# One pair of PSUM pools for the whole program, and the way down over output tiles q and 4 + q

## The chip, the cores and the metric

The kernel runs on one core of a Trainium2 chip. The metric is the device time of one execution in microseconds (us). The kernel before takes 1079.97 us in the median of three runs (1079.96 to 1080.04).

## The reference

One layer of a hybrid decoder on a sequence of 1024 positions of width 1024, all in float32. A mixer (a short convolution on 512 channels, chunkwise retention with four heads on the others) is followed by a squared-ReLU network; both add to the residual stream, and a norm ends the layer:

```python
for _ in range(DEPTH):
    h = h + hybrid_mixer(rms_norm(h, norm1_g), w_in, conv_w, conv_norm_g, ret_norm_g, w_out)
    h = h + sq_relu_mlp(rms_norm(h, norm2_g), w_up, w_down)
return rms_norm(h, final_norm_g)

def sq_relu_mlp(u, w_up, w_down):
    hdn = jax.nn.relu(u @ w_up)
    return (hdn * hdn) @ w_down
```

`w_up` is 1024 x 4096 and `w_down` 4096 x 1024.

## The kernel before

Everything is held transposed: features on the 128 partitions, the 1024 positions along the columns, in two halves of 512 (`hs[0]` low, `hs[1]` high). The residual stream is eight tiles `x2[0..7]` of 128 x 1024, one for each 128 features.

**Matmuls.** float32 operands are split in a high part and the rest (`wh`, `wl` for weights, `U`, `V`, `hid` for the moving side), and a product is three matmuls for each block of 128 features: high by high, high by rest, rest by high. ACT casts the high part, DVE (sometimes POOL) subtracts for the rest. A product of four blocks is 12 matmuls of 512 columns into one PSUM bank; the code is `mm` (line 395), `product` (772) and, for the way down, `down_product` (1266).

**Fewer products.** Both matrix products of the network use a scheme of seven products instead of eight (Winograd's form of Strassen's), on 2 x 2 blocks of weights and data. The sums of weight blocks are made on POOL (`r<-r,r` in the profile, from `Left.split`), those of data blocks on DVE and POOL. For the way down, the four quarters of a 2 x 2 block of outputs are two tiles of `x2` by two halves of the positions. The seven products are added straight into these quarters by DVE (`down_take`, line 1277), in a basis in which fewer additions are needed. For that the residual has to be put in the basis first (`new_basis`, line 1001, two subtractions on POOL for each pair of tiles) and taken out at the end (one addition to each of the two tiles, lines 1316 and 1346). Before the change, the pairs are neighbours: (0, 1), (2, 3), (4, 5), (6, 7).

**Stages around the change.** The program is recorded by hand (a manual schedule): each engine runs its instructions in the order of the code, and waits are put in where data or buffers need them.

1. Output projection, `group(j)` (1057), j = 0 to 3: eight products each, for output tiles j and 4 + j. The finished tiles go to `x2` (`out_evac`), and the network's input blocks are made from them, step by step (`group_todo`, 1035; a step is one product, the table `todo` counts 8 steps to a group). Tiles of `x2` that are not needed for a while are written to HBM (`put_aside`, 1025; `k<-x` on SP's queue) and later read back (`fetch_back`, 1031; `x<-k`).
2. The early products (1248): the 14 products of the first two pairs of up blocks, without a way down beside them. The table `rest` says what is issued beside each. The norm's roots are matmuls with a column of ones (L311), and the rows are spread over the partitions with L337 into two banks that are kept for the rest of the program (`r_half`).
3. The loop (1328): up products (L401) and down products (L1274) in turn, then the last block of `w_down` and the final norm (1377 on).

**Banks.** PSUM has eight banks for this kernel. Up to the end of the projection two pools, `pm` and `pr`, have four each. Then both are closed and three are opened: two banks for the up products (`pu`, which takes the name `pm`), four for the down products (`pd`, taking the name `pr`), two for the norm rows (`pn`). A bank is given again when the last reader of its old tile is done.

In the profile nearly all work of DVE, ACT and POOL has line L74, since one helper records it; the tiles' names tell the operations apart: `x<-x,b` adds a bank to the residual, `t<-t,b` adds an up product, `wl<-r,wh` is the rest of a weight piece, `U<-un,U` and `V<-t,V` the rest of a data block, `x<-x,x` and `x<-x` the two subtractions of `new_basis`, `t<-t,t` on POOL sums of squares (before 452 us) or sums of data blocks.

Of the kernel before, what the change touches and what calls it, by code (L numbers as in the profile page):

```python
# [14 lines left out]
PSUM = bass.MemoryType.PSUM  # L15
# [64 lines left out]
def hybrid_layer(  # L80
# [18 lines left out]
    pool = Engine(nc.gpsimd, 0.2, 2.5, now, clock)  # L99
# [5 lines left out]
    rw = ctx.enter_context(tc.tile_pool(name="rw", bufs=4))  # L105
    wp = ctx.enter_context(tc.tile_pool(name="wp", bufs=4))
    mixer = ctx.enter_context(ExitStack())
    banks_ = ctx.enter_context(ExitStack())
    pm = banks_.enter_context(tc.tile_pool(name="pm", bufs=4, space=PSUM))
    pr = banks_.enter_context(tc.tile_pool(name="pr", bufs=4, space=PSUM))  # L110
    tp = mixer.enter_context(tc.tile_pool(name="tp", bufs=6))
    xp = mixer.enter_context(tc.tile_pool(name="xp", bufs=1))

# [4 lines left out]
    def nm(s):  # L118
        n_[0] += 1
        return f"{s}{n_[0]}"  # L120

    def unit(dt=F32, s="u"):
        return big.tile([P, T], dt, tag="u", name=nm(s))
# [6 lines left out]
    def bank(pool_=None):  # L130
        return (pool_ or pm).tile([P, H], F32, tag="b", name=nm("b"))
# [4 lines left out]
    hs = [slice(0, H), slice(H, T)]  # L136
# [196 lines left out]
    def spread(wide, pool_=None):  # L333

        b = bank(pool_ or pr)[:, : len(wide) * P]
        for c, d in enumerate(wide):
            nc.tensor.matmul(b[:, c * P : (c + 1) * P], d, ident, start=True, stop=True)  # L337
        return b
# [201 lines left out]
    def rot_tiles(ct, st):  # L540

        ac, as_ = unit(s="ac"), unit(s="as")

        def evac_a(A):
            for half, sl in enumerate(hs):
                dve.tensor_mul(ac[:, sl], A[half], ct[:, sl])
                dve.tensor_mul(as_[:, sl], A[half], st[:, sl])

        tile_in(evac_a)
        q = [unit(s="q") for _ in range(2)]  # L550

        def evac(B):
            for half, sl in enumerate(hs):
                t2, t3 = tmp(), tmp()
                dve.tensor_mul(t2, B[half], st[:, sl])
                dve.tensor_mul(t3, B[half], ct[:, sl])
                lo_, up_ = slice(0, 64), slice(64, 128)
                pool.tensor_sub(q[0][lo_, sl], ac[lo_, sl], t2[lo_])
                dve.tensor_sub(q[1][lo_, sl], ac[up_, sl], t2[up_])
                dve.tensor_add(q[0][up_, sl], t3[lo_], as_[lo_, sl])  # L560
                pool.tensor_add(q[1][up_, sl], t3[up_], as_[up_, sl])

        tile_in(evac)
        return q
# [189 lines left out]
    for p in range(2):  # L754
        q = rot_tiles(*ropes)
# [11 lines left out]
    def put_hi(name, j, src):  # L767
        u = unit(F32R, "U")
        act.copy(u[:, :H], src)
        U.setdefault(name, [None] * 4)[j] = (u[:, :H], u[:, H:])  # L770
# [44 lines left out]
    for j in range(4):  # L815
        for c, name in ((0, "11"), (1, "21"), (2, "22")):
            k = j + (4 if c else 0)
            sl = hs[c == 2]
# [119 lines left out]
    x2 = [unit(s="x2") for _ in range(KT)]  # L938
# [59 lines left out]
                un[i] = unit(s="un")  # L998
            act.activation(un[i][:, hs[half]], x, AF.Copy, scale=g)

    def new_basis(i):


        for f, part in ((i - 1, hs[1]), (i, hs[0])):
            pool.tensor_sub(x2[f][:, part], x2[f][:, part], x2[i][:, hs[1]])

# [16 lines left out]
    def put_aside(i):  # L1025

        aside[i] = kept.tile([P, T], F32, tag="k", name=nm("k"))
        nc.sync.dma_start(aside[i], x2[i])
        x2[i] = None
# [5 lines left out]
    def group_todo(j):  # L1035

        hi_of = lambda *names: [lambda x=x: put_hi(x, j, source(x, j)) for x in names]
        lo_of = lambda *names: [lambda x=x: put_lo(x, j, source(x, j)) for x in names]
        todo = {
            2: [lambda: put_scaled_hi("11", j, j, 0)],  # L1040
            3: [lambda: put_scaled_lo("11", j, j, 0)],
            4: [lambda: put_scaled_hi("21", j, 4 + j, 0)],
            5: [lambda: put_scaled_lo("21", j, 4 + j, 0)],
            8: [lambda: sum1(j)] + hi_of("t1"),
            9: lo_of("t1") + [lambda: sum3(j)],
            10: [lambda: sum2(j)],
        }
        if j < 3:
            todo[10] += hi_of("t3")
            todo[11] = lo_of("t3") + hi_of("t2")  # L1050
            todo[12] = lo_of("t2") + [lambda: put_scaled_hi("22", j, 4 + j, 1)]
            todo[13] = [lambda: put_scaled_lo("22", j, 4 + j, 1), lambda: sum4(j)] + hi_of("t4")
            todo[14] = lo_of("t4")
            todo[15] = [lambda: put_aside(4 + j)]
        return todo

    def group(j):
# [27 lines left out]
    todo = {}  # L1085
    for j in range(4):
        for at, fs in group_todo(j).items():
            todo.setdefault(8 * j + at, []).extend(fs)
    todo[16] += [lambda: new_basis(1)]
    todo[17] += [lambda: put_aside(0), lambda: put_aside(1)]  # L1090
    todo[24] += [lambda: put_aside(2)]
    for j in range(4):
        group(j)
    banks_.close()
    pm = ctx.enter_context(tc.tile_pool(name="pu", bufs=2, space=PSUM))
    pr = ctx.enter_context(tc.tile_pool(name="pd", bufs=4, space=PSUM))
    pn = ctx.enter_context(tc.tile_pool(name="pn", bufs=2, space=PSUM))

    blocks = [w_up[p, i] for p in range(EARLY, NP_) for i in range(4)]
    blocks += [w_last[i] for i in range(KT)]  # L1100
# [45 lines left out]
    r_half, waiting = [None, None], []  # L1146
# [42 lines left out]
    def v_split(pairs, n, j):  # L1189
        c = pairs[j].c  # L1190
        src = c[{1: "11", 2: "21", 3: "22", 4: "21", 5: "11", 6: "11", 7: "12"}[n]]
        u = unit(F32R, "V")
        act.copy(u[:, :H], src)
        eng = pool if j and n not in (2,5) else dve
        eng.tensor_sub(u[:, H:], src, f32(u[:, :H]))
        V.setdefault(n, [None] * 2)[j] = (u[:, :H], u[:, H:])
# [26 lines left out]
    def call(f, *js):  # L1223
        return [lambda j=j: f(j) for j in js]
# [4 lines left out]
    def lo22(j):  # L1229
# [7 lines left out]
        lo("t4", dve, 3) + call(fetch_back, 2, 4, 5, 6),  # L1237
        [],
        [],
        call(new_basis, 7),  # L1240
        call(new_basis, 5),
        call(new_basis, 3),
        [lambda: v_split(early, 1, 0)],
        [lambda: v_split(early, 1, 1)],
        [],
# [2 lines left out]
    for at, (n, p) in enumerate((n, p) for n in MLP_ORDER for p in range(EARLY)):  # L1248
        b = early[p].product(n)
        if at == 0:  # L1250
            up.fetch(4)
        prepare()
        for f in rest[at]:
            f()
        put_now()
        early[p].take(n, b)
        if at == 3:
            roots = [token_roots([sums_[h]], rtok[:, 4 * h : 4 * h + 4]) for h in range(2)]
        if at == 5:
            wides = [rnorms(r) for r in roots]  # L1260
        if at == 8:
            r_half[:] = [spread(w, pn) for w in wides]
        while r_half[0] is not None and waiting:
            waiting.pop(0)()

# [11 lines left out]
    def down_take(n, h, bs):  # L1277
        for i, b in enumerate(bs):
            q = 2 * h + i
            quads = [x2[2 * q + f][:, sl] for f in range(2) for sl in hs]  # L1280
            for to, op in {
                1: ((0, ALU.add), (3, ALU.add)), 2: ((0, ALU.add),), 3: ((1, ALU.add),),
                4: ((2, ALU.add),), 5: ((2, ALU.subtract), (3, ALU.add)), 6: ((3, ALU.add),),
                7: ((1, ALU.subtract), (3, ALU.add)),
            }[n]:
                dve.tensor_tensor(quads[to], quads[to], b, op)
# [11 lines left out]
    def jobs(b, old, new):  # L1298

        todo = []  # L1300
        for k, n in enumerate(DOWN_ORDER):
            four = [[] for _ in range(4)]
            if k < 6:
                for j in range(2):
                    four[j].append(lambda n=DOWN_ORDER[k + 1], j=j: v_split(old, n, j))
                    four[j + 1].append(lambda n=DOWN_ORDER[k + 1], j=j: v_next(old, n, j))
            elif b < NBLK - 2:
                for j in range(2):
                    four[j].append(lambda j=j: v_both(new, 1, j))
            if b == NBLK - 2:  # L1310
                late = {4: ((0, "11"), (0, "21"), (0, "12"), (0, "22")), 5: ((1, "11"),)}.get(k, ())
                for f, x in zip(four, late):
                    f.append(lambda x=x: last_split(*x))
                if k == 6:
                    for q in range(4):
                        x = x2[2 * q + 1]
                        four[q].append(
                            lambda x=x: pool.tensor_add(x[:, hs[0]], x[:, hs[0]], x[:, hs[1]])
                        )
                    for f, name in ((four[0], "12"), (four[2], "22"), (four[3], "21")):  # L1320
                        f.append(lambda name=name: last_split(1, name))
            todo += four
        return todo
# [4 lines left out]
    for b in range(NBLK - 1):  # L1328
        new = [Pair(pm), Pair(pm)]
        todo = jobs(b, pairs, new)  # L1330
# [12 lines left out]
            else:  # L1343
                pairs[x].take(y, bk)
    for q in range(4):
        pool.tensor_add(x2[2 * q][:, hs[1]], x2[2 * q][:, hs[1]], x2[2 * q + 1][:, hs[1]])


    wd = []
# [27 lines left out]
    for sl in (slice(0, 512), slice(512, 768), slice(768, 1024)):  # L1377
# [3 lines left out]
        for i in range(KT):  # L1381
# [21 lines left out]
            x = x2[i][:, sl]  # L1403
# [120 lines left out]
```

## Time and profile before

| | |
|---|---|
| median of 3 runs | 1079.97 us |
| the profiled execution | 1082.14 us |
| its span (first to last instruction) | 1080.3 us |
| granted TensorE clock, mean | 0.995 |
| output projection on PE | 353.7 to 440.6 us |
| early products | 441 to 484 us |
| loop, then last block and final norm | 484 to 1022, to 1080 us |

DVE is TensorE's companion at 82% of the span, but in the second half of it the page's 40 slices show DVE at 90% or more nearly everywhere. A row of the timeline gives the start and the length in us, the engine, the line, the tile written and the tiles read, the shapes and a count, and in brackets the idle time ahead of it with what ended it. A row of the groups gives a count, the busy time and the mean in ns. A row of the windows gives the busy time of PE, of its weight loads, of DVE, ACT and POOL in a stretch, then the granted clock.

### The profile page before, as it was taken

To read this page: it belongs to the slowest core of one execution; us is meant where nothing else is said; L and a number is where in the kernel's file an instruction comes from. 1 tells how busy PE (TensorE), PEld (TensorE's weight loads), DVE (VectorE), ACT (ScalarE), POOL (GpSimd) and SP (SyncE) were. 2 spreads that over 40 slices of the span, in tenths; PEclk is the share of its full clock that TensorE was granted. 3 is DMA by queue.
4 is the path that set the end of the run, shared out by engine and by line. 5 is a ranking of instruction groups with operands and counts; after the bars stand their busy time and mean duration, and the time that the engine had idled before them with its cause. 6 is when DMAs were issued, how large, how long until landed. Compare 5 with 4: busy or idle time off the path is not lost.

```text
span 1080.3 us, 14040 instructions
## 1 busy us (share of the span) xinstructions
PE 1060.6 (98%) x4936; PEld 882.7 (82%) x4936; DVE 881.2 (82%) x1255; ACT 463.3 (43%) x916; POOL 540.3 (50%) x370
## 2 busy tenths in 40 slices
PE   9999999999999999999999999999999999999996
PEld 7888888887778888788788888888888888888886
DVE  8446546799997666699999989999899899899945
ACT  8211445763335544444343443443343434334453
POOL 6233323256752132559548258267286295384543
PEclk9999999999999999999999999999999999999998
DMA  7121121212223635050121211211301211210204
GB/s 273 62 59 48 31 79 69 100 58 77 69 59 117 224 114 169 2 194 30 58 69 39 79 39 49 89 25 54 93 25 50 88 30 43 85 30 12 77 1 157
DMA packets 40311, 81.75 MB, mean 76 GB/s; under 512 B 4528, under 2 KB 6704, under 8 KB 40240
## 3 DMA queue, kind: packets, MB, share of 16 engines
q1 hardware_dynamic: 40240, 80.85, 23.2%
q8 instruction: 39, 0.64, 0.2%
q14 instruction: 32, 0.26, 0.1%
HBM read 71.40 MB, written 9.44 MB: 75 GB/s over the span
## 4 chain that ended last, share of the span: by engine, by line
PE 80%; DVE 11%; issue 3%; POOL 3%; ACT 2%; DMA 1%; POOLq 0%; DVEq 0%; SPq 0%; ACTq 0%
PE b L401 50%; PE b L1274 23%; PE b L355 4%; DVE z L74 2%; DVE wl L74 2%; POOL r L74 1%; POOL z L74 1%; DVE t L74 1%; DVE x L74 1%; DVE xs L74 1%; DVE U L74 1%; DVE q L74 1%; ACT h L74 1%; PE b L337 1%; DVE m L74 1%
## 5 line engine op out<-in xcount | busy, mean ns | idle before, releaser
L401 PE MATMUL b<-U,wh 128*128 128x512 f32 x1024 | 315.9, 390 | 2.4 <-DVE x L74 1.2
L74 ACT CAST wh<-r 128x512 fp32r<-128x512 f32 x286 | 175.9, 620 | 321.2 <-PE b L401 134.7
L74 DVE TENSOR_TENSOR wl<-r,wh 128x512 fp32r<-128x512 f32 x251 | 233.3, 932 | 90.9 <-ACT wh L74 90.0
L74 POOL TENSOR_TENSOR r<-r,r 128x512 f32<-128x512 f32 x136 | 209.8, 1545 | 116.0 <-DVE wl L74 65.6
L1274 PE MATMUL b<-V,wh 128*128 128x512 f32 x784 | 242.0, 389 | 0.7 <-POOL V L74 0.4
L401 PEld LDWEIGHTS b<-U,wh 128*128 128x128 f32 x1024 | 191.8, 188 | 43.4 <-issue 2.8
L74 DVE TENSOR_TENSOR x<-x,b 128x512 f32<-128x512 f32 (+1 forms) x320 | 197.8, 663 | 24.4 <-PE b L401 19.3
L401 PE MATMUL b<-U,wl 128*128 128x512 f32 x512 | 199.4, 389 | 0.0
L1274 PEld LDWEIGHTS b<-V,wh 128*128 128x128 f32 x784 | 147.0, 188 | 32.3 <-POOL V L74 0.8
L74 POOL TENSOR_TENSOR t<-t,t 128x512 f32<-128x512 f32 x70 | 106.3, 1523 | 97.9 <-ACT t L74 51.9
L1274 PE MATMUL b<-V,wl 128*128 128x512 f32 x392 | 152.5, 389 | 0.0
L74 POOL TENSOR_TENSOR wl<-r,wh 128x512 fp32r<-128x512 f32 x35 | 49.1, 1408 | 159.2 <-ACT wh L74 151.9
L401 PEld LDWEIGHTS b<-U,wl 128*128 128x128 f32 x512 | 96.0, 188 | 20.7 <-POOL wl L74 0.4
L401 PE MATMUL b<-uh,wh 128*128 128x512 f32 x304 | 103.3, 399 | 2.3 <-DVE z L74 2.3
L401 PE MATMUL b<-uh,wl 128*128 128x512 f32 x304 | 100.8, 392 | 1.1 <-DVE wl L74 1.1
L401 PE MATMUL b<-ul,wh 128*128 128x512 f32 x304 | 101.0, 392 | 0.0
L1274 PEld LDWEIGHTS b<-V,wl 128*128 128x128 f32 x392 | 73.6, 188 | 15.2
L74 POOL TENSOR_TENSOR V<-t,V 128x512 fp32r<-128x512 f32 x35 | 49.6, 1417 | 67.2 <-ACT V L74 67.2
L74 DVE TENSOR_TENSOR t<-t,b 128x512 f32<-128x512 f32 x112 | 75.8, 677 | 1.7 <-POOL t L74 1.2
L74 ACT ACTIVATE t<-t 128x512 f32<-128x512 f32 x64 | 40.2, 631 | 81.9 <-DVE t L74 81.3
L74 DVE TENSOR_TENSOR V<-t,V 128x512 fp32r<-128x512 f32 x63 | 70.3, 1116 | 0.0
L401 PEld LDWEIGHTS b<-uh,wl 128*128 128x128 f32 x304 | 57.3, 189 | 13.9 <-DVE wl L74 1.5
(168 smaller groups left out, 1431.0 us busy)
## 6 DMA issues: line engine op xcount, KB each, us to landing
r<-w_up_t SPq DMA_DIRECT2D x64, 256.0 KB, 2.6
r<-w_down_t SPq DMA_DIRECT2D x56, 256.0 KB, 2.7
r<-w_in_t SPq DMA_DIRECT2D x48, 256.0 KB, 2.6
xt<-xT SPq DMA_DIRECT2D x16, 256.0 KB, 5.4
xs<-xT SPq DMA_DIRECT2D x8, 512.0 KB, 4.8
r<-w_out_t SPq DMA_DIRECT2D x16, 256.0 KB, 2.7
x<-xT SPq DMA_DIRECT2D x8, 512.0 KB, 7.4
k<-x SPq DMA_DIRECT2D x6, 512.0 KB, 3.2
```

What stands on the lines that cost most here:

```text
L74: return f(out, *args, **kw)
L337: nc.tensor.matmul(b[:, c * P : (c + 1) * P], d, ident, start=True, stop=True)
L355: nc.tensor.matmul(vb[i], a[k][:, i * P : (i + 1) * P], b[k // 2][:, vs], start=(k == 0 and a is uh and b is vh), stop=(k == KT - 1 and a ...
L401: nc.tensor.matmul(b, a[:, k, :], rhs(n, k)[r], start=(start and i == 0), stop=(stop and i == len(ops) - 1),)
L1274: nc.tensor.matmul(b, a, r, start=(i == 0), stop=(i == len(ops) - 1))
```

## The change

The two pools `pm` and `pr` of four banks stay for the whole program; the norm rows take two banks of `pm`. The way down pairs output tiles q and 4 + q instead of 2q and 2q + 1: these come from the same group of the projection, so `new_basis(j)` can stand behind the group's own steps, at step 14 (which is six products into the next group), and tiles j and 4 + j are put aside together at step 15. Only the last pair (3, 7), which is never put aside, stays in the early products. The columns of `w_down` are laid out on the host to match.

```diff
-    banks_ = ctx.enter_context(ExitStack())
-    pm = banks_.enter_context(tc.tile_pool(name="pm", bufs=4, space=PSUM))
-    pr = banks_.enter_context(tc.tile_pool(name="pr", bufs=4, space=PSUM))
+    pm = ctx.enter_context(tc.tile_pool(name="pm", bufs=4, space=PSUM))
+    pr = ctx.enter_context(tc.tile_pool(name="pr", bufs=4, space=PSUM))
...
-    def new_basis(i):
-        for f, part in ((i - 1, hs[1]), (i, hs[0])):
-            pool.tensor_sub(x2[f][:, part], x2[f][:, part], x2[i][:, hs[1]])
+    def new_basis(j):
+        for f, part in ((j, hs[1]), (4 + j, hs[0])):
+            pool.tensor_sub(x2[f][:, part], x2[f][:, part], x2[4 + j][:, hs[1]])
...
             todo[14] = lo_of("t4")
-            todo[15] = [lambda: put_aside(4 + j)]
+            todo[14] += [lambda: new_basis(j)]
+            todo[15] = [lambda: put_aside(j), lambda: put_aside(4 + j)]
...
-    todo[16] += [lambda: new_basis(1)]
-    todo[17] += [lambda: put_aside(0), lambda: put_aside(1)]
-    todo[24] += [lambda: put_aside(2)]
...
-    banks_.close()
-    pm = ctx.enter_context(tc.tile_pool(name="pu", bufs=2, space=PSUM))
-    pr = ctx.enter_context(tc.tile_pool(name="pd", bufs=4, space=PSUM))
-    pn = ctx.enter_context(tc.tile_pool(name="pn", bufs=2, space=PSUM))
...
-        call(new_basis, 7),
-        call(new_basis, 5),
         call(new_basis, 3),
+        [],
+        [],
...
-            r_half[:] = [spread(w, pn) for w in wides]
+            r_half[:] = [spread(w, pm) for w in wides]
...
-            quads = [x2[2 * q + f][:, sl] for f in range(2) for sl in hs]
+            quads = [x2[4 * f + q][:, sl] for f in range(2) for sl in hs]
...
-                        x = x2[2 * q + 1]
+                        x = x2[4 + q]
...
-        pool.tensor_add(x2[2 * q][:, hs[1]], x2[2 * q][:, hs[1]], x2[2 * q + 1][:, hs[1]])
+        pool.tensor_add(x2[q][:, hs[1]], x2[q][:, hs[1]], x2[4 + q][:, hs[1]])
```

Where instructions move, on POOL, at the end of the projection and in the first four early products (`t_3190` sums squares, `r` are weight blocks, `x_3164` and `x_3168` are x2[2] and x2[6]; a piece of the difference):

```order
 L74 TENSOR_TENSOR t_3190<-t_3190,t_3846 128x512
-L74 TENSOR_TENSOR r_3594<-r_3594,r_3596 128x512
-L74 TENSOR_TENSOR r_3590<-r_3594,r_3590 128x512
-L74 TENSOR_TENSOR r_3592<-r_3592,r_3590 128x512
-L74 TENSOR_TENSOR t_3190<-t_3190,t_3871 128x512
+L74 TENSOR_TENSOR x_3164<-x_3164,x_3168 128x512
+L74 TENSOR_TENSOR x_3168<-x_3168 128x512
+L74 TENSOR_TENSOR r_3592<-r_3592,r_3594 128x512
+L74 TENSOR_TENSOR r_3588<-r_3592,r_3588 128x512
+L74 TENSOR_TENSOR r_3590<-r_3590,r_3588 128x512
+L74 TENSOR_TENSOR t_3190<-t_3190,t_3873 128x512
```

The two subtractions of the pair (2, 6) come in ahead of the three weight sums and of the last addition of squares (`t_3190`), which are otherwise the same.

On POOL again, later in the early products, before the change (`x_4037` and `x_3169` are x2[6], read back, and x2[7]; the next two pairs are (4, 5) and (2, 3); `V_4214` is a data block of the first down product):

```order
L74 TENSOR_TENSOR r_3594<-r_3596,r_3590 128x512
L74 TENSOR_TENSOR x_4037<-x_4037,x_3169 128x512
L74 TENSOR_TENSOR x_3169<-x_3169 128x512
L74 TENSOR_TENSOR x_4033<-x_4033,x_4035 128x512
L74 TENSOR_TENSOR x_4035<-x_4035 128x512
L74 TENSOR_TENSOR x_4031<-x_4031,x_3165 128x512
L74 TENSOR_TENSOR x_3165<-x_3165 128x512
L74 TENSOR_TENSOR V_4214<-t_3997,V_4214 128x512
```

And at the same place now (`x_3165` and `x_3169` are x2[3] and x2[7], neither of them read back):

```order
L74 TENSOR_TENSOR r_3410<-r_3412,r_3406 128x512
L74 TENSOR_TENSOR r_3592<-r_3594,r_3588 128x512
L74 TENSOR_TENSOR x_3165<-x_3165,x_3169 128x512
L74 TENSOR_TENSOR x_3169<-x_3169 128x512
L74 TENSOR_TENSOR V_4203<-t_3990,V_4203 128x512
```

Four of the six subtractions have gone from here, and none of the two left reads a tile that comes back from HBM.

On PE, at the first early product, with the engines that the program waits for, before:

```order
L401 MATMUL b_3804<-yh_3080,wl_3697 128x512
L401 MATMUL b_3887<-U_3249,wh_3795 128x512 [waits DVE_49,PE_49,Activation_49]
L401 MATMUL b_3887<-U_3249,wh_3795 128x512
L401 MATMUL b_3887<-U_3249,wl_3796 128x512
L401 MATMUL b_3887<-U_3404,wh_3795 128x512 x2
```

and now:

```order
L400 MATMUL b_3804<-yh_3080,wl_3697 128x512
L400 MATMUL b_3880<-U_3249,wh_3795 128x512 [waits Activation_49]
L400 MATMUL b_3880<-U_3249,wh_3795 128x512
L400 MATMUL b_3880<-U_3249,wl_3796 128x512 [waits DVE_49]
L400 MATMUL b_3880<-U_3404,wh_3795 128x512 x2
```

The first row is the projection's last matmul. The product's first wait for DVE (and for PE's own last product) is gone, and a wait for DVE stands at the first use of `wl`; the second early product changes in the same way.

More of the change, by code (lines that the diff above doesn't have):

```diff
@@ L1502 @@
         .reshape(NBLK - 1, 2, 2, P, 2, 2, 2, P)
-        .transpose(0, 6, 2, 4, 3, 5, 1, 7)
+        .transpose(0, 4, 2, 5, 3, 6, 1, 7)
         .reshape(NBLK - 1, 4, 2, P, 4, P),
```

## The prediction

> **What bounds the kernel now.** I read the page's busy times first, then TensorE's (PE's) idle gaps in order of time, then the engines that end them.
>
> ```profile
> span 1080.3 us, 14040 instructions
> PE 1060.6 (98%) x4936; PEld 882.7 (82%) x4936; DVE 881.2 (82%) x1255; ACT 463.3 (43%) x916; POOL 540.3 (50%) x370
> 529.98 2.72 PE b L401 x12
> ```
>
> PE is busy for 98% of the span. A product of the program is 12 matmuls of 512 columns, and in the chain of work that ended last one takes 2.72 us, or 0.23 us a matmul. The time can fall only where PE is kept from this pace, and rise only where a new wait breaks it. Between 332 us (the output projection's start) and 988 us the timeline has five gaps on PE, all between 440 and 525 us, which is where the change acts.
>
> The first two, from the timeline of PE:
>
> ```profile
> 440.39 0.39 PE L401 MATMUL b<-yh,wl 128*128 128x512 f32 x1
> 441.25 0.70 PE L401 MATMUL b<-U,wh 128*128 128x512 f32 x2 [0.47 <-DVE x L74]
> 443.82 0.39 PE L401 MATMUL b<-U,wl 128*128 128x512 f32 x1
> 444.91 0.70 PE L401 MATMUL b<-U,wh 128*128 128x512 f32 x2 [0.70 <-DVE x L74]
> 447.75 0.39 PE L401 MATMUL b<-U,wh 128*128 128x512 f32 x1
> ```
>
> The last projection matmul starts at 440.39, so the first early product was due at 440.62 and the third at 440.62 + 2 x 2.72 = 446.06. It starts at 447.75: **1.69 us lost**. Both waits end with DVE's `x += b`, which empties a projection bank. The program's waits agree: these two matmuls alone name DVE and PE beside ACT, because the pools are closed there and new ones laid over the same banks.
>
> The other three:
>
> ```profile
> 494.92 0.39 PE L401 MATMUL b<-U,wh 128*128 128x512 f32 x1
> 506.44 0.70 PE L401 MATMUL b<-U,wh 128*128 128x512 f32 x2 [0.48 <-ACT wh L74]
> 520.54 0.70 PE L1274 MATMUL b<-V,wh 128*128 128x512 f32 x2 [0.25 <-DVE x L74]
> 524.25 0.70 PE L401 MATMUL b<-U,wh 128*128 128x512 f32 x2 [0.71 <-ACT t L74]
> 527.10 0.39 PE L1274 MATMUL b<-V,wh 128*128 128x512 f32 x1
> L401 PE MATMUL b<-U,wh 128*128 128x512 f32 x48 | 15.0, 393 | 1.2 <-ACT t L74 0.7 <-ACT wh L74 0.5
> 505.62 0.67 DVE L74 TENSOR_TENSOR t<-t,b 128x512 f32<-128x512 f32 x1
> 523.43 0.68 DVE L74 TENSOR_TENSOR t<-t,b 128x512 f32<-128x512 f32 x1
> ```
>
> From 494.92 to 527.10 there are 32.18 us. The group row, of this window, counts 48 `U,wh` matmuls, 8 to an up product, so six up products and the five down products between them: 11 x 2.72 = 29.92. **2.26 us lost.** The profile names ACT, but the bank decides: an up product needs the bank of the up product before last, and DVE frees those with the two `t<-t,b`, at 506.29 and 524.11, just ahead of the gaps' ends. DVE lags PE here; 0.6 to 0.9 us less lag would end these gaps.
>
> **Why DVE lags.**
>
> ```profile
> 473.71 1.28 POOL L74 TENSOR_TENSOR x<-x,x 128x512 f32<-128x512 f32 x1 [12.17 <-DMA x<-k]
> 482.56 1.76 POOL L74 TENSOR_TENSOR V<-t,V 128x512 fp32r<-128x512 f32 x1
> 479.10 0.62 ACT L74 CAST V<-t 128x512 fp32r<-128x512 f32 x1
> 473.79 1.76 DVE L74 TENSOR_TENSOR wl<-r,wh 128x512 fp32r<-128x512 f32 x1 [0.90 <-ACT wh L74]
> 478.42 1.78 DVE L74 TENSOR_TENSOR V<-t,V 128x512 fp32r<-128x512 f32 x1
> 474.00:484.00 10.00, 10.00 (x45) 8.29 (x45) 9.90 (x11) 5.29 (x10) 10.00 (x7) 1.00 0.25 74
> 451.22 0.69 DVE L74 TENSOR_TENSOR wl<-r,wh 128x512 fp32r<-128x512 f32 x1 [2.30 <-ACT wh L74]
> ```
>
> The six `new_basis` subtractions of the late pairs fill POOL from 473.71 to 482.56, after 12.17 us of waiting for a tile from HBM. Meanwhile DVE's `wl` takes 1.76 us, and 0.69 at 451.22 with POOL idle. From 474 to 484 both engines count as busy throughout (9.90 and 10.00). A POOL operation alone takes 1.28, beside DVE 1.74; a DVE operation with both inputs in SBUF that meets one ends about 0.6 behind it. Those that read a bank (`t<-t,b`, 0.67) don't mind.
>
> **The change, part by part.**
>
> *The banks.* Without close and reopen, the first early products take banks emptied groups ago and wait for weights alone (split before 440). Both gaps go: **-1.69 us**. In the loop nothing changes: the norm rows now sit in two of `pm`'s four banks, leaving two for the up products, as before.
>
> *The new order on POOL.* The count is the same (8 subtractions). Two pairs move ahead of 440. From 335 to 440 PE is busy for all of 105 us and POOL for 32.27 (first row below), so I cost them at nothing. The third pair (x2[2], x2[6]) lands in the busiest place:
>
> ```profile
> 335.00:440.00 105.00, 105.00 (x465) 86.95 (x464) 67.66 (x91) 49.98 (x86) 32.27 (x22) 1.00 0.39 131
> ...
> 441.88 1.74 POOL L74 TENSOR_TENSOR t<-t,t 128x512 f32<-128x512 f32 x1
> 443.58 4.80 POOL L74 TENSOR_TENSOR r<-r,r 128x512 f32<-128x512 f32 x3
> 448.33 1.74 POOL L74 TENSOR_TENSOR t<-t,t 128x512 f32<-128x512 f32 x1
> 451.83 0.68 DVE L74 TENSOR_TENSOR U<-un,U 128x512 fp32r<-128x512 f32 x1
> 452.44 1.41 DVE L74 SCALAR_TENSOR_TENSOR un<-x,sm,un 128x512 f32<-128x512 f32 x2
> 455.53 0.69 DVE L74 TENSOR_TENSOR wl<-r,wh 128x512 fp32r<-128x512 f32 x1 [1.69 <-ACT wh L74]
> 456.14 0.68 DVE L74 TENSOR_TENSOR U<-un,U 128x512 fp32r<-128x512 f32 x1
> 453.19 1.84 PE L311 MATMUL b<-ones,t 128*128 128x1 f32 x16
> 457.07 0.62 PE L401 MATMUL b<-U,wh 128*128 128x512 f32 x2
> ```
>
> Behind the `t` at 441.88 two subtractions go in, one beside DVE and one alone (1.74 + 1.28 = 3.0), so the three `r` and the last sum `t` run 3.0 later: `t` ends at 450.07 + 3.0 = 453.1. Two things wait for that. The sums on PE (L311), due at 453.19 - 1.69 = 451.50, need `t` for their second half. And DVE: with POOL idle from 450.07 it ran `U` at 451.83 in 0.68; now `U` meets `t` and ends 0.6 behind it, 453.7 instead of 452.5, **1.2 late**. The two `un`, ACT's `U`, `t` and `wh`, then `wl` and `U` (456.14) follow one another without slack, so the last `U`, low half of the fourth tile of "t2", ends at 456.82 + 1.2 = 458.0. The tenth and eleventh matmuls of product 6 of pair 0 (457.07 and 457.30) use that tile, the eleventh its low half; it had 0.5 to spare and now runs at 458.05, 0.75 later than before. So PE waits there until all of the 1.69 is gone and **0.75 us more**: bounds are 0 after the gain (the stretch hidden) and +2.8 (DVE loses the turn at U and both `un`, 3 x 1.1, less 0.5). I take 0.75, by the rows themselves. The roots at L311 are hidden under this wait.
>
> For this cost the Trainium skill has a rule: SBUF — State Buffer, section "SBUF: two separate sides", says of the port pair that DVE and GpSimd share that it is "an exclusive lock, not a bandwidth split", held for the whole instruction. The two full rows of 474 to 484 agree. If the engines shared evenly instead, `U` and what follows would be some 0.6 late instead of 1.2, and the sum below would be 0.6 lower; the rule speaks against this place for the pair.
>
> *The last pair* (x2[3], x2[7]) never leaves SBUF, so it doesn't wait for HBM: it follows the `r` of 459.81, at about 462.7 to 466.
>
> ```profile
> 459.81 1.74 POOL L74 TENSOR_TENSOR r<-r,r 128x512 f32<-128x512 f32 x1 [1.83 <-DVE wl L74]
> 463.32 0.69 DVE L74 TENSOR_TENSOR wl<-r,wh 128x512 fp32r<-128x512 f32 x1 [0.63 <-ACT wh L74]
> 466.37 0.39 PE L401 MATMUL b<-U,wl 128*128 128x512 f32 x1
> ```
>
> DVE's `wl` of 463.32 may lose 1.2 to the chain above and 1.1 to this pair; it ends at 464.01, PE uses it at 466.37 and comes 0.75 later too, so 3.1 us hide it. I cost it at nothing; without that cover it would be up to 1.1.
>
> *What goes after 473.* POOL is empty until `V`, which starts when ACT's `V` is there (479.72, and 0.75 later with PE): 480.5 instead of 482.56, 2.1 earlier. On DVE two `wl` and a `V` between 473.79 and 480 shrink by 1.1 each, 3.3; it comes there some 1.6 later (the 1.2, and part of the pair at 463), so it is 1.7 ahead. With PE 0.75 later its lag is 2.4 less, against 0.9 needed. The three gaps go: **-2.26 us**, bounds 0 and 2.26.
>
> *Queues and tail.* SP's writes of x2[2] and x2[6] now wait for POOL until about 446, and four `w_up` loads stand behind them:
>
> ```profile
> 422.55 1.91 SPq L160 DMA_DIRECT2D r<-w_up_t  x4
> 475.90 0.63 ACT L74 CAST wh<-r 128x512 fp32r<-128x512 f32 x1 [0.56 <-ACT t L74]
> 1022.62 6.40 POOL L74 TENSOR_TENSOR x<-x,x 128x512 f32<-128x512 f32 x4
> 1044.30 0.42 DVE L74 TENSOR_TENSOR x<-x,b 128x256 f32<-128x256 f32 x1 [0.75 <-POOL ssq L74]
> ```
>
> They are issued at about 447 instead of 422.55 and used first at 475.90: hidden, with over 20 us left. In the tail, POOL's four closing additions end at 1029 and their half is read from 1044.30: nothing either way.
>
> **The sum.** -1.69 + (1.69 + 0.75) - 2.26 = -1.5 us. The profiled execution took 1082.14 (span 1080.3), the runs 1079.97 in the median; 1.5 off gives 1080.6 for such an execution and **1078.5** for the median. A measurement here tells about 0.2%, 2.16 us, from no change.
>
> **Rivals.**
> - *The pair on POOL is hidden.* If POOL gets through by 451.8 or DVE goes first, product 6 doesn't wait: -1.69 - 2.26 = -3.95, 1076.0. For it: 0.5 us of spare at 457.30, and durations on POOL are rough. Against it: POOL has no idle time from 440.64 to 450.07 to take 3.0 in.
> - *The lag stays.* DVE is full from 474 to 515 whatever runs beside it; if `V` and the `r` on POOL only close up, the gaps at 506 to 524 remain: +0.75, 1080.7.
> - *Slower.* The same lock, lost at `U` and both `un`, which needs POOL busy until 456: +2.8 at 457.30, and with DVE that much behind the later gaps stay: 1082.8. It decides from the point where the eleventh matmul of product 6 starts after 459.5 by the old clock. Against it: behind `t` POOL's next `r` waits for DVE's own `wl` (455.53).
> - *The banks were not the wait.* Then 441 and 444 stay, but PE waits for the same `U` at 458.05 and the sum is -1.5 again.
>
> **Chances.** Forecast (with the last rival) 0.52, own range 1077.6 to 1079.6; hidden 0.20; lag stays 0.18; slower 0.10. The range 1075.8 to 1081.4 takes in all but the slower case and the far ends. Faster by over 0.2%: the hidden case and a little of the forecast, 0.26; within: 0.64; slower: 0.10.
>
> **What would show it.** PE without gaps at 441 and 444, then one gap of 1.5 to 2.5 us inside product 6 put down to DVE's `U`, and none from 500 to 527; POOL with `x` rows near 443.6 and 463 and none at 473 to 482; `t` ending near 453. It is wrong if product 6 doesn't wait, if the gaps at 506 to 524 stand, or if PE stops anywhere in 332 to 440 or in the tail where it didn't.

## The result, and the profile after

| | before | after |
|---|---|---|
| median | 1080.34 us (20 runs) | 1082.55 us (20 runs) |
| the profiled execution | 1082.14 us | 1081.98 us |
| its span | 1080.3 us | 1080.2 us |

The ratio of the times is 1.0017, interval [1.0011, 1.0024]: about 0.2% **slower**, where 0.14% faster was forecast. The two profiled executions took the same time, so they can't be compared as wholes: before's lies 1.8 us above its median. They can be compared stretch by stretch, between matmuls that both kernels have. From the timeline of PE, after (columns as above):

```profile
318.33 0.50 PE L400 MATMUL b<-uh,wh 128*128 128x512 f32 x1 [2.29 <-DVE z L74]
438.62 0.39 PE L400 MATMUL b<-yh,wl 128*128 128x512 f32 x1
449.50 0.39 PE L400 MATMUL b<-U,wl 128*128 128x512 f32 x1
449.73 0.95 PE L310 MATMUL b<-ones,t 128*128 128x1 f32 x8
453.72 1.86 PE L310 MATMUL b<-ones,t 128*128 128x1 f32 x8 [3.04 <-POOL t L74]
455.44 1.20 PE L400 MATMUL b<-U,wh 128*128 128x512 f32 x2
...
459.43 0.82 PE L400 MATMUL b<-U,wh 128*128 128x512 f32 x2
489.33 0.62 PE L1267 MATMUL b<-V,wh 128*128 128x512 f32 x2
1061.42 0.28 PE L310 MATMUL b<-ones,ssq 128*128 128x1 f32 x2
```

And the same places before, as far as not shown yet:

```profile
318.60 0.80 PE L401 MATMUL b<-uh,wh 128*128 128x512 f32 x1 [2.27 <-DVE z L74]
486.76 0.62 PE L1274 MATMUL b<-V,wh 128*128 128x512 f32 x2
1061.09 0.28 PE L311 MATMUL b<-ones,ssq 128*128 128x1 f32 x2
```

| stretch, from start to start | before | after | |
|---|---|---|---|
| z's matmul to the projection's last matmul | 121.79 | 120.29 | -1.50 |
| to the first down product (**early stretch**) | 46.37 | 50.71 | +4.34 |
| to the final norm's sums at 1061 (**the rest**) | 574.33 | 572.09 | -2.24 |

The first row is not the change: in before's execution PE ran at half pace for 3.4 us behind its wait for z (0.80 us for the first matmul in its row, 0.50 after). That came and went from profile to profile, whatever the kernel (last section). The other two rows add up: +4.34 - 2.24 = +2.1 us, which is the difference of the medians, 2.2. So the gain that was hoped for behind the early products came, and the early products lost twice as much.

What PE does there, from the windows of after:

```profile
440.00:460.00 20.00, 16.96 (x71) 14.23 (x70) 13.85 (x14) 8.26 (x15) 13.83 (x9) 0.83 0.31 107
500.00:527.00 27.00, 27.00 (x121) 22.37 (x120) 25.74 (x37) 10.82 (x19) 20.74 (x14) 1.00 0.20 59
452.50:453.00 0.50, 0.00 (x0) 0.00 (x0) 0.50 (x2) 0.00 (x0) 0.50 (x1) 1.00 0.68 262
453.00:453.50 0.50, 0.00 (x0) 0.00 (x0) 0.50 (x1) 0.00 (x0) 0.50 (x1) 0.51 0.07 25
```

The gaps at 441 and 445 are gone, and so are those from 500 to 527 (27.00 of 27.00). In their place PE stands still for 3.04 us at the roots, behind the last sum of squares `t`. While it stands the granted clock falls from 1.00 to 0.50 (at 453.0; it is back before 460), so that product 6, which follows, starts at half pace.

Behind that stop, ACT, DVE, POOL and SP of after:

```profile
427.32 0.61 ACT L74 CAST U<-un 128x512 fp32r<-128x512 f32 x1
431.34 0.73 ACT L74 ACTIVATE U<-x,sm 128x512 fp32r<-128x512 f32 x1 [3.41 <-PE b L400]
431.97 0.61 ACT L74 ACTIVATE t<-x 128x512 f32<-128x512 f32 x1
434.50 1.78 DVE L74 TENSOR_TENSOR U<-un,U 128x512 fp32r<-128x512 f32 x1
436.20 1.78 DVE L74 TENSOR_TENSOR wl<-r,wh 128x512 fp32r<-128x512 f32 x1
452.47 1.75 DVE L74 TENSOR_TENSOR U<-un,U 128x512 fp32r<-128x512 f32 x1
457.83 0.68 DVE L74 TENSOR_TENSOR U<-un,U 128x512 fp32r<-128x512 f32 x1
433.99 3.44 POOL L74 TENSOR_TENSOR r<-r,r 128x512 f32<-128x512 f32 x2
451.95 1.71 POOL L74 TENSOR_TENSOR t<-t,t 128x512 f32<-128x512 f32 x1
420.60 27.01 SPq L1027 DMA_DIRECT2D k<-x  x4
```

and of before, at the first and the last of these places:

```profile
429.60 0.72 ACT L74 ACTIVATE U<-x,sm 128x512 fp32r<-128x512 f32 x1
430.66 0.63 ACT L74 ACTIVATE t<-x 128x512 f32<-128x512 f32 x1 [0.34 <-DVE x L74]
434.89 0.68 DVE L74 TENSOR_TENSOR U<-un,U 128x512 fp32r<-128x512 f32 x1
408.30 13.85 SPq L1028 DMA_DIRECT2D k<-x  x3
```

The last row, DVE's `U` of 457.83, is the `U` of product 6 on which the prediction turned. It ends at 458.51, 19.89 us behind the start of the projection's last matmul (438.62); before it ended at 456.82, 16.43 behind 440.39. So it is **3.46 us later, where 1.2 was forecast**. One part is the forecast one (`U` at 452.47 takes 1.75 beside POOL, not 0.68). The other starts twenty microseconds earlier: ACT's `U<-x,sm` waits 3.41 us, with the square `t` behind it in ACT's queue; POOL's weight sums `r`, which follow that square's addition, come later for it and meet DVE's `U` and `wl` (1.78 each). That `U` of 434.50 ends at -2.34 us from the projection's last matmul, where before's, of 434.89, ended at -4.82: 2.5 us of the delay are there already, before POOL's two subtractions begin.

### The profile page after: what moved, and what is told of

Its sections match the earlier page's. It is cut to its first block, busy times and chain, and to the rows that moved or that the text cites. A ratio compares the mean times of both kernels' runs of the same rounds, so it can differ in the third digit from the quotient of the medians.

```text
span 1080.2 us, 14041 instructions
## 1 busy us (share of the span) xinstructions
PE 1061.0 (98%) x4936; PEld 884.6 (82%) x4936; DVE 882.9 (82%) x1255; ACT 463.8 (43%) x916; POOL 541.3 (50%) x370
## 4 chain that ended last, share of the span: by engine, by line
PE 85%; DVE 6%; POOL 4%; issue 3%; ACT 1%; DMA 0%; POOLq 0%; DVEq 0%; ACTq 0%
PE b L400 53%; PE b L1267 24%; PE b L354 4%; POOL r L74 1%; POOL z L74 1%; DVE z L74 1%; DVE wl L74 1%; DVE q L74 1%; DVE t L74 1%; PE b L336 1%; PE b L310 1%; PE b L622 0%; PE b L592 0%; DVE cv L74 0%; ACT h L74 0%
## 5 line engine op out<-in xcount | busy, mean ns | idle before, releaser
L74 DVE TENSOR_TENSOR V<-t,V 128x512 fp32r<-128x512 f32 x63 | 68.1, 1081 | 0.0
```

What stands on the lines that cost most here:

```text
L74: return f(out, *args, **kw)
```

## The experiments

The theory at first was the stop at the roots; the rival, that the chain of DVE and ACT to the last `U` of product 6 decides, wherever PE is seen to stand. Below, "U" is the end of that `U` and "early" the start of the first down product, both from the start of the projection's last matmul; "rest" is as in the table above. These three come from one profiled execution of each kernel (before again shows how far two of one kernel differ: 0.6), the ratio from 11 or 12 runs, in basis at 15 from 5, in the change from 20.

| kernel | U | early | rest | early + rest against before | ratio of times |
|---|---|---|---|---|---|
| before | 16.43 | 46.37 | 574.33 | | |
| before again | 16.44 | 46.37 | 573.75 | -0.6 | |
| banks only | 16.47 | 46.15 | 574.86 | +0.3 | 0.9999 [0.9990, 1.0008] |
| aside late | 16.49 | 46.14 | 574.55 | 0.0 | 0.9994 [0.9985, 1.0003] |
| pairs only | 19.96 | 50.46 | 572.11 | +1.9 | 1.0018 [1.0008, 1.0028] |
| the change | 19.89 | 50.71 | 572.09 | +2.1 | 1.0017 [1.0011, 1.0024] |
| basis at 15 | 20.02 | 52.57 | 572.13 | +4.0 | 1.0033 [1.0021, 1.0046] |
| basis late | 18.92 | 50.04 | 572.11 | +1.5 | 1.0021 [1.0012, 1.0030] |
| u11 late | 17.58 | 47.24 | 572.11 | -1.3 | 0.9995 [0.9986, 1.0004] |
| slot | 17.41 | 48.65 | 572.10 | +0.1 | 0.9999 [0.9990, 1.0008] |
| all | 17.42 | 48.70 | 572.07 | +0.1 | 1.0002 [0.9993, 1.0011] |
| banks, lo | 15.20 | 44.87 | 574.51 | -1.3 | 0.9986 [0.9977, 0.9996] |
| best | 15.29 | 46.34 | 572.10 | -2.3 | 0.9984 [0.9974, 0.9994] |
| best 2 | 15.27 | 46.34 | 572.06 | -2.3 | 0.9982 [0.9971, 0.9993] |

**Before again.**

> The kernel before once more, for a second profile of it. Its first one had a fallen clock from 318 to 322 us (granted 0.54 to 0.61, about 1.5 us lost) behind PE's 2.27 us wait for z, which the changed kernel's profile did not have. Theory: that is chance, and an execution without it takes about 1080.0 to 1080.4 and reaches the end of the projection near 438.7 as the changed kernel does. Rival: the fallen clock belongs to the kernel before, and shows again. The gaps from 506 to 524 (2.26 us in the prediction) are seen again if they belong to the program; if not, the prediction's third term was never there to gain.

It took 1080.84 us, early stretch as in the first profile, and the half pace behind z was there again. The later gaps are there too, a little smaller (rest 573.75): the third term of the prediction was a real thing to gain, though its size differs between executions. Whether before takes about 1080.0 without the half pace could not be seen in this execution.

**Banks only**: the pools of the change, before's pairs.

```diff
-    banks_ = ctx.enter_context(ExitStack())
-    pm = banks_.enter_context(...); pr = banks_.enter_context(...)
+    pm = ctx.enter_context(...); pr = ctx.enter_context(...)
...
-    banks_.close()
-    pm = ...; pr = ...; pn = ...
```

> Only the pools: before's pairs, but the two pools of four banks stay. Theory (the stop at the roots costs, by POOL's order): no gaps at 441 and 445, the last sum of squares ends about 450 as before, the roots find it ready or nearly, and the time falls by 0.4 to 1.7 us against before (1.3 us of it may come back in product 6, since its last U ended at 456.8 and PE would want it at 455.5). Rival (DVE's and ACT's chain to that U sets the time, whatever the banks do): PE waits there or at the roots for as long as the gaps were, and the time is before's within 0.3 us. Rival (the banks layout itself costs): slower than before by 2 us.

Nothing was gained. Its timeline of PE shows why:

```profile
438.63 0.39 PE L400 MATMUL b<-yh,wl 128*128 128x512 f32 x1
449.74 1.84 PE L310 MATMUL b<-ones,t 128*128 128x1 f32 x16
455.16 0.51 PE L400 MATMUL b<-U,wh 128*128 128x512 f32 x1 [1.14 <-DVE U L74]
```

No gap until the roots, no wait at them, and 1.14 us in product 6 for DVE's `U`. The gaps at the banks had only stood where PE would have waited anyway. The rival holds here.

**Pairs only**: the change with before's pools, closed and opened again.

> Only the pairing: tiles q and 4+q with the change of basis in the groups, but the pools closed and opened as before. Theory (the stop at the roots): gaps at 441 and 445 hold PE back by about 1.7 us or more, so the stop at the roots is 3.0 less that, 0.5 to 1.4 us, too short for the clock to fall; the time is before's +0 to +1 us, below the changed kernel's by 1.5 or more. Rival (the chain to the last U sets the time): as the changed kernel, +2.2 against before, with the same clock loss.

It is as slow as the change. PE stands 2.94 us at the first bank, 0.69 at the next and 0.46 in product 6 for `U`, and not at the roots; the `U` is as late as in the change. This is the rival's case but for the clock, which did not fall here: the place of the stop moved, the loss stayed. (0.55 us of it is a stop for ACT's `wh` at 469.42, which the change does not have.) It also shows that the pairing alone brings the rest to 572.1, and that the loss is the pairing's.

**Basis at step 15**: POOL's two subtractions behind the last sum of squares.

```diff
-            todo[14] += [lambda: new_basis(j)]
-            todo[15] = [lambda: put_aside(j), lambda: put_aside(4 + j)]
+            todo[15] = [lambda: new_basis(j), lambda: put_aside(j), lambda: put_aside(4 + j)]
```

> The changed kernel with new_basis(j) one step later (step 15, behind the group's last sum of squares on POOL instead of ahead of it). Theory (the stop at the roots): the last sum ends at 450.1 to 450.8, the 3.04 us stop at the roots and the slow clock after it are gone, and the time falls by 2 to 5 us against the changed kernel, below before by 0 to 2. Rival (the last U of product 6 decides): PE passes the roots, and stops in product 6 for DVE's U, which meets the two subtractions and ends at 458 to 459, by 3 to 4.5 us; the clock falls there in its place and the time stays within 0.5 us of the changed kernel's.

The slowest of all. From its timelines of PE and DVE:

```profile
457.75 0.49 PE L400 MATMUL b<-U,wh 128*128 128x512 f32 x1 [2.27 <-ACT U L74]
460.08 0.80 PE L400 MATMUL b<-U,wh 128*128 128x512 f32 x1 [1.84 <-DVE U L74]
461.10 1.05 PE L400 MATMUL b<-U,wh 128*128 128x512 f32 x2
453.94 1.78 DVE L74 TENSOR_TENSOR U<-un,U 128x512 fp32r<-128x512 f32 x1
```

PE passes the roots and stands in product 6 instead, for ACT's and DVE's halves of the same `U`, and the clock falls there (two matmuls in 1.05 us, not 0.62). The theory of the stop at the roots is out. What was open now: why is the `U` 3.46 us late, when the subtractions beside it account for 1.1?

**Aside late**: banks only, with `x2[2]` put aside at step 31 instead of 24.

```diff
-    todo[24] += [lambda: put_aside(2)]
+    todo[31] += [lambda: put_aside(2)]
```

> The banks-only kernel (before's pairs), with one thing more: x2[2] is put aside at step 31 instead of 24, as the pairing has it. Theory (a buffer of the 1024-column tiles comes free later, so ACT's U<-x,sm for the last group waits for PE's last read of a projection input, with the sum of squares and two more U behind it in ACT's queue): ACT waits some 3.4 us in one piece near 428 to 431, POOL's r collide with DVE's U and wl, the last U of product 6 ends about 18.9 us after the projection's last matmul starts instead of 16.5, PE stops about 3.8 us at the roots or in product 6 instead of 1.3, and the time is 2 to 4 us above banks-only. Rival (only POOL's two subtractions make that U late): as banks-only within 0.3 us.

A miss: no effect. The queue of SP shows that the edit had hardly moved the write:

```profile
406.70 14.33 SPq L1027 DMA_DIRECT2D k<-x  x3
428.01 0.72 ACT L74 ACTIVATE U<-x,sm 128x512 fp32r<-128x512 f32 x1
```

The last write is issued by 421.0, as before, since SP's queue is not held by the steps of the code but by its data and by what stands ahead in it. The write of `x2[2]` only changed places with that of `x2[6]` (420.60, in banks only 416.87), well ahead of the `U` that ACT wants at 428. In the change the data hold it: the write of `x2[2]` waits for POOL's subtraction and is issued at 446.05, where it was issued at 418.63, and the last write at 447.3 (SP's row of after above). So its buffer is free some 27 us later. The addresses in the programs show who wanted it: in before, banks only and aside late the `U` for which ACT waits in the change lies where `x2[2]` lay; in the change and in all kernels with the pairing it lies on a tile `yl`, an operand of the projection that PE has yet to read. The next experiments move the demand for the buffer, or the subtractions, and not a place in the code.

**Slot**: the change, with two `U` moved that ask for buffers at that time: 11 of the last group from steps 26 and 27 to 28 and 29, 22 of the third group to step 31.

```diff
+        if j == 3:
+            todo[4] = todo.pop(2) + todo[4]
+            todo[5] = todo.pop(3) + todo[5]
...
-            todo[12] = lo_of("t2") + [lambda: put_scaled_hi("22", j, 4 + j, 1)]
-            todo[13] = [lambda: put_scaled_lo("22", j, 4 + j, 1), lambda: sum4(j)] + hi_of("t4")
+            q22 = [lambda: put_scaled_hi("22", j, 4 + j, 1), lambda: put_scaled_lo("22", j, 4 + j, 1)]
+            todo[12] = lo_of("t2") + (q22[:1] if j < 2 else [])
+            todo[13] = (q22[1:] if j < 2 else []) + [lambda: sum4(j)] + hi_of("t4")
...
-            todo[15] = [lambda: put_aside(j), lambda: put_aside(4 + j)]
+            todo[15] = (q22 if j == 2 else []) + [lambda: put_aside(j), lambda: put_aside(4 + j)]
```

> The changed kernel with the demand for that buffer moved: the U of 11 for the last group from steps 26 and 27 to 28 and 29, the U of 22 for the third group from 28 and 29 to 31. Theory (the buffer): ACT's square follows its x at once again, the last U ends about 17.5 us after the projection's last matmul instead of 19.9, the last sum of squares about 12.6 after it, the stop at the roots is under 0.7 us, product 6 waits about 2 us, the clock does not fall, and the time is 2 to 3.5 us below the changed kernel, about before's. Rival (only the two subtractions count): the U moves by less than 0.5 and the time stays the changed kernel's.

The `U` came to 17.41 and the time to before's: the buffer was 2.5 us of the delay. No fall of the clock was expected behind PE's stop in product 6; it stood 1.83 us, and there was one.

**U11 late**: the first of those two moves only, the cleanest form. (Its diff is the first three lines of the one above.)

> The changed kernel with only the U of 11 of the last group moved, from steps 26 and 27 to 28 and 29, behind the square and the U that wait behind it in ACT's queue. POOL's subtractions stay where they are. Theory (buffer wait 2.4, subtractions 1.1): the last U ends at 17.5 to 17.8 after the projection's last matmul, the first down product starts at 47.2 to 47.6 (48.7 if the clock falls), and the time is before's or up to 1 us below it. Rival (subtractions the whole delay): the U stays at 19.9, the first down product at 49.5 to 50.7, and the time is the changed kernel's.

**Basis late**: the other half alone. POOL's pair (2, 6), with its writes, moves beside the sixth early product; the buffer still comes free late.

```diff
+            if j < 2:
                 todo[14] += [lambda: new_basis(j)]
                 todo[15] = [lambda: put_aside(j), lambda: put_aside(4 + j)]
...
-        lo("t4", dve, 3) + call(fetch_back, 2, 4, 5, 6),
-        [],
-        [],
+        lo("t4", dve, 3) + call(fetch_back, 4, 5),
+        call(new_basis, 2) + call(put_aside, 2, 6),
+        call(fetch_back, 2, 6),
```

> The changed kernel with the pair (2, 6) alone moved: new_basis(2) and putting x2[2] and x2[6] aside stand beside the sixth early product, and they are read back beside the seventh. POOL's two subtractions are then not ahead of the last sum of squares, nor beside DVE's U; but x2[2]'s buffer comes free late, as in the changed kernel. Times from the start of the projection's last matmul: Theory (most of the U's delay is the wait for a buffer, 2.4 us, the subtractions beside it only 1.1): no stop at the roots; the last U ends at 18.4 to 19.0 (16.45 before, 19.9 changed), PE stops 3 to 4 us in product 6, the first down product starts at about 49.5, later if the clock falls; the time is 0.5 to 1.5 us below the changed kernel. Rival (the subtractions on POOL are the whole delay): the U ends at 16.5, the first down product starts at 46.2 and the time is some 4 us below the changed kernel, 2 below before.

U11 late came out as its theory had it. Basis late did so for the `U` and for PE's stops (1.20 us for ACT's half, 1.83 for DVE's), but not for the time: the clock fell, the first down product came at 50.04, and its ratio can't be told from the change's. For the `U`, the two together divide the delay. From the timelines of u11 late:

```profile
430.55 0.63 ACT L74 ACTIVATE t<-x 128x512 f32<-128x512 f32 x1 [0.94 <-DVE x L74]
451.81 1.75 DVE L74 TENSOR_TENSOR U<-un,U 128x512 fp32r<-128x512 f32 x1
457.18 0.69 DVE L74 TENSOR_TENSOR U<-un,U 128x512 fp32r<-128x512 f32 x1
453.07 1.05 PE L310 MATMUL b<-ones,t 128*128 128x1 f32 x8 [0.73 <-POOL t L74]
457.92 0.50 PE L400 MATMUL b<-U,wh 128*128 128x512 f32 x1 [1.37 <-DVE U L74]
```

and of basis late:

```profile
431.53 0.73 ACT L74 ACTIVATE U<-x,sm 128x512 fp32r<-128x512 f32 x1 [3.22 <-PE b L400]
452.75 0.68 DVE L74 TENSOR_TENSOR U<-un,U 128x512 fp32r<-128x512 f32 x1
457.79 0.79 PE L400 MATMUL b<-U,wh 128*128 128x512 f32 x1 [1.83 <-DVE U L74]
```

With the buffer's wait gone, the first `U` still takes 1.75 and the last ends 17.58 behind: 1.15 later than before. With the subtractions gone the first `U` takes 0.68 again, ACT's wait stands at 3.22, and the last `U` ends 18.92 behind: 2.49 later. 1.15 + 2.49 = 3.64, against 3.46 for both.

**All**: slot, with `new_basis(j)` at step 13, and the low part of "t1" with its two sums beside the first early product:

```diff
     rest = [
-        todo[32] + call(hi22, 3),
-        todo[33] + todo[34] + hi("t2", 3),
+        todo[32] + todo[33] + todo[34],
+        hi("t2", 3) + call(hi22, 3),
```

> As e6_slot, and new_basis(j) one step earlier (step 13, into the 3.9 us in which POOL waits), and the low part of t1 and the two sums behind it for the last group issued beside the first early product instead of the second, ahead of DVE's wait for the next weights. Theory (the chain of DVE and ACT to the last U of product 6 is what PE waits for, in one place or another): that U ends before 15.1 us after the projection's last matmul, PE passes the early products with under 0.5 us lost, none is lost from 500 to 527, and the time is 1.5 to 3 us below before. Rival (another chain is next, the sum of squares for the roots or the t4 of the next products): PE stops there, and the time is within 0.5 of before.

A miss. The subtractions met other operations of DVE (436 to 449), and what the earlier "t1" gained was lost there: the `U` ended 17.42 behind, as in slot.

**Banks, lo**: banks only, with that last edit.

> Banks-only (before's pairs), with the low part of t1 and the two sums issued beside the first early product as in e8_all. Theory (the chain to the last U): the U ends about 14.2 us after the projection's last matmul instead of 16.5, product 6 does not stop, and the time falls by 1 to 1.7 us against before. Rival (PE coming earlier only meets DVE's lag at 500 to 527): the gaps there grow by as much and the time is before's within 0.3.

The `U` ends 15.20 behind (14.2 was expected), PE does not wait for it at all, and the early stretch is 44.87: 1.3 us below banks only, with a rest like before's. This shows by the other sign that the `U` was what PE waited for.

**Best**: both moves (u11 late, basis late) and the earlier "t1".

> Both moves of e12_basis_late and e11_u11_late, and the low part of t1 with its two sums beside the first early product as in e9_banks_lo. Theory: the last U ends at 14.5 to 15.2, the first down product starts at 44.9 (46.4 before, 44.87 in e9_banks_lo), and from there to the final norm's sums it is 572.1 us as with the pairing (574.3 before): 3.7 us below before, about 0.34%. Rival (POOL's two subtractions, now at about 457, or the late reading back of x2[2] and x2[6], give DVE its lag back or stop the first products of the way down): 574 or more from there on, and the time is that of e9_banks_lo, 0.14% below before.

0.16% below before, half of what was expected. From its timelines of PE and DVE:

```profile
468.22 2.05 PE L336 MATMUL b<-ident,t 128*128 128x128 f32 x16 [1.09 <-DVE t L74]
463.54 1.78 DVE L74 TENSOR_TENSOR U<-un,U 128x512 fp32r<-128x512 f32 x1
```

The `U` is in time, but now PE stands 1.09 us for the norm rows: POOL's four subtractions run from 460.07 to 466.5 and slow DVE on its way to them (the `U` of this fence takes 1.78, in banks, lo 0.69).

**Best 2**: the same with the four subtractions written behind the norm rows.

```diff
-        call(new_basis, 2) + call(put_aside, 2, 6),
-        call(fetch_back, 2, 6),
-        call(new_basis, 3),
-        [],
-        [],
+        [],
+        [],
+        [],
+        call(new_basis, 2) + call(put_aside, 2, 6),
+        call(new_basis, 3) + call(fetch_back, 2, 6),
```

> As e10_best, with both late pairs' subtractions on POOL moved behind the norm rows (beside the ninth and tenth early products; they ran from 460.07 to 466.5 there, and DVE's wl and U beside them took 1.73, 1.78 and 1.18 us where they take 0.69 in e9_banks_lo, so that PE stopped 1.09 us for the norm rows' t). Theory: that stop goes, the first down product starts at 44.9 to 45.3 after the projection's last matmul instead of 46.34, the rest stays 572.1, and the time is 1 to 1.4 us below e10_best, about 0.27% below before. Rival (POOL beside DVE from 470 to 477 makes DVE lag at 500 to 527 again, as the kernel before had it): the rest grows back to 573.5 or more, and the time is e10_best's or above.

A miss: the edit left the subtractions where they were. POOL of best 2:

```profile
458.86 1.74 POOL L74 TENSOR_TENSOR r<-r,r 128x512 f32<-128x512 f32 x1 [1.83 <-DVE wl L74]
460.56 1.74 POOL L74 TENSOR_TENSOR x<-x,x 128x512 f32<-128x512 f32 x1
479.98 1.73 POOL L74 TENSOR_TENSOR V<-t,V 128x512 fp32r<-128x512 f32 x1 [13.02 <-ACT V L74]
```

POOL has nothing else between the `r` of 458.86 and the `V` of 479.98, so the subtractions run directly behind the `r` wherever the code puts them between the two. Best, best 2 and banks, lo are all below before and below the change (0.14 to 0.18%); their intervals overlap, and which of them is best is open.

## Why the prediction was wrong

- **Banks, -1.69, given back in product 6.** Right. (332 us, where the prediction has the projection start, is 21 us ahead of it, which changes no term.) The gaps went, and banks only shows that the `U` of product 6 takes the place of nearly all of it: the early stretch falls by 0.22 and the time by nothing.
- **The pair (2, 6) on POOL, +0.75 in all.** Right in mechanism and size, as far as it went. The prediction had `t` and `U` pushed, the roots hidden and the last `U` 1.2 late, ending 458.0 - 440.39 = 17.6 behind the projection's last matmul, and an early stretch of 46.37 + 0.75 = 47.12. In u11 late, where only this acts, they are 17.58 and 47.24. The trace agrees with the rule drawn on there (the Trainium skill, SBUF — State Buffer, section "SBUF: two separate sides"): in the change `U` meets POOL's `t` (451.95 to 453.66) and ends 0.56 behind it, at 454.22.
- **The two pairs ahead of 440: nothing.** Right. From z's matmul to the projection's last it is 120.29 us in the change and 120.27 in banks only, both at full clock.
- **Queues: "SP's writes of x2[2] and x2[6] now wait for POOL until about 446 ... hidden".** This step failed. The time of the writes was right (446.05 and 447.3), and so was that of the loads (from 447.7), but the prediction asked only for the loads that stand behind them in SP's queue. It didn't ask which buffer a write sets free and who takes it: ACT's next `U`. It put at nothing what was the largest term. That `U` waited 3.41 us, the chain behind it met POOL's sums, and the last `U` was 2.3 to 2.5 us later still (basis late: 2.49 of it alone).
- **The clock.** Not in the prediction. Where the clock did not fall and PE waited for the `U` (banks only, aside late, u11 late), the early stretch is the `U` plus 29.65 to 29.68. For the change that makes 19.89 + 29.66 = 49.55; it took 50.71, so the half pace behind the stop cost 1.2 us beyond the late `U`. Slot (48.65 against 17.41 + 29.66) and basis late lose 1.5 to 1.6 in the same way. These are differences between kernels: pairs only, at full clock, lies 0.8 above its `U` plus 29.66, with other stops.
- **Last pair at 463: nothing.** Right for the change. Best shows how thin that cover was: with PE on time, this pair and (2, 6) in front of it cost 1.09 there.
- **Later gaps, -2.26.** Right: the rest fell by 2.24, and to 572.1 in every kernel with the pairing. That it met 2.26 so closely is in part luck: against before again (573.75) it is 1.66.
- **The sum.** Forecast +0.75 - 2.26 = -1.5; measured +4.34 - 2.24 = +2.1. The 3.6 between them are 2.3 for the `U` (19.89 against 17.6), 1.2 for the clock, and 0.1. The rival "slower" had its place right (the `U`) and its mechanism wrong: DVE lost one turn to POOL there, not three (`un` and `un` took 1.40). That its 1082.8 lies so near the measured 1082.55 is luck, since it counts the later gaps, which went.
- **What was to show it.** The gap in product 6 put down to `U` is not to be seen in the change: the stop at the roots and the half pace let PE come late enough. Whoever reads only the largest wait in the list (POOL's `t`, 3.04) takes the symptom for the cause, as the first theory did; basis at 15 took that stop away and lost more.

## What to carry to other kernels

When a step is put behind another, ask not only what stands behind it in its queue but which buffer its end sets free and who is given that buffer next. Where several engines run ahead of one another, a place in the code holds an operation back only by what stands ahead of it on its own engine, and by its data, as aside late and best 2 showed. And find the cause of a stop by the offset of the late operand from a fixed point, not by the wait at which the profile happens to show it; here one offset orders the kernels, but for what the clock took from some of them, whose stops stand at several places.

## What was not expected of the hardware

The granted clock fell to 0.50 behind short stops of PE, and not always behind long ones. At the wait for z, 2.27 to 2.32 us in all fourteen profiles, it fell in ten and not in four, and the stretch to the projection's end was 121.8 to 121.9 us with it and 120.3 without: 1.6 us. It fell behind 1.83 us in slot, and not behind 2.94 in pairs only. Once fallen, it stayed for 3.4 us (before, 318.5 to 321.85; slot, 458.3 to 461.7) or twice that (after, 453.0 to 459.8). From the windows of slot:

```profile
459.00:460.00 1.00, 1.00 (x3) 0.75 (x3) 1.00 (x2) 0.00 (x0) 0.00 (x0) 0.50 0.59 158
461.50:462.00 0.50, 0.50 (x4) 0.39 (x3) 0.50 (x1) 0.50 (x1) 0.50 (x2) 0.81 0.00 0
```

What looks like chance has a rule in these traces. Twelve of the profiles have two falls or more behind 200 us (the last in the final norm), and there the falls start a whole number of windows of 3.413 us apart: in slot at 318.33, 458.27 and 1072.67, 41 and 180 windows. On that grid, carried on through each profile, the wait for z leaves PE standing for 2.00 to 2.32 us of one window in the ten that fell, and for at most 1.85 (the change) in the four that did not. Slot's 1.83 lie whole in one window; the 2.94 of pairs only are parted by an edge, at 441.82, into 1.52 and 1.42. So between matmuls of 512 columns the turn lies near 1.84 us of standing within one window, and what varies is where the windows lie against the program. (In the final norm, among matmuls of one column, 0.88 were enough in pairs only.)

The Trainium skill, TensorE: Matmul & The Clock Gate, section "Part 1: The HAM clock gate (the "warmup" mystery)", has the clock halved after at least one idle window of about 3.4 us, and the windows run freely, not from the kernel's start. The lengths here, in steps of 3.4, and the grid agree with such windows; that a window must be idle throughout does not, since in slot PE was busy for 1.58 of the 3.41 us ahead of the fall.
